# Adaptive max-pooling over rows in a ring: one VectorE instruction per three-row load instead of one per row

## Chip, cores and metric

The kernel runs on one core of one Trainium2 chip. The metric is device time in microseconds (us) of that core. A run over 1.5% above the fastest of its kernel is called slow, the others fast.

## Reference

The input has 32 x 256 rows of 4096 fp32 numbers. Every row is cut into 256 windows of 16, and the maximum of each window is the output: 134.2 MB are read and 8.4 MB written.

```python
def reference(x, output_size):          # x: (32, 256, 4096), output_size = 256
    result = np.zeros((batch, channels, output_size), dtype=np.float32)
    for i in range(output_size):
        start = int(i * length / output_size)
        end = int((i + 1) * length / output_size)
        result[:, :, i] = np.max(x[:, :, start:end], axis=-1)
    return result
```

## The kernel before

Each of the 128 partitions handles 64 rows. 63 of them come in 21 loads of three rows (6 MB over all partitions); the last comes alone in a 2 MB load. The rows go round a ring with nine slots, so three loads fit: one being pooled, two in flight or queued. The results stay on the chip in three `outs` tiles and are stored at the end. Everything except the last small store is issued by one queue (SP), in program order. A load that reuses slots waits, before it is issued, for the pooling that read those slots.

```python
    RING = 9
    G = 21
    N_GROUPS = 3
    LOAD = 3
    CUT = 15
    # ... (tiles ring [P, RING, O, W] and outs[0..2] [P, G * O]; views xg, og, xl, ol)

    def pooled(dst, src):
        nc.vector.reduce_max(out=dst, in_=src, axis=mybir.AxisListType.X)

    n_read = 0
    for g in range(N_GROUPS):
        for r in range(0, G, LOAD):
            at = n_read % RING
            nc.sync.dma_start(
                out=ring[:, at : at + LOAD], in_=xg[g][:, r : r + LOAD]
            )
            for i in range(LOAD):
                pooled(outs[g][:, (r + i) * O : (r + i + 1) * O], ring[:, at + i])
            n_read += LOAD

    at = n_read % RING                    # 63 % 9 = 0: first slot of a trio
    spare = ring[:, (at + LOAD) % RING].rearrange("p o w -> p (o w)")[:, 0:O]
    nc.sync.dma_start(out=ring[:, at], in_=xl)
    pooled(spare, ring[:, at])

    for g in range(N_GROUPS - 1):
        nc.sync.dma_start(out=og[g], in_=outs[g])
    for a, b in ((0, CUT), (CUT, G)):
        nc.sync.dma_start(
            out=og[N_GROUPS - 1][:, a * O : b * O],
            in_=outs[N_GROUPS - 1][:, a * O : b * O],
        )
    nc.scalar.dma_start(out=ol, in_=spare)
```

## Time and profile before

| What | Before |
|---|---|
| time, median of the first 3 runs | 335.93 us |
| VectorE busy | 278.8 us, 83% of the span |
| one load to the next | 14.53 us |
| pooling of one load, three instructions | 13.07 us |
| VectorE idle before each load's pooling | 1.46 us |
| DMA in the steady stretch | share 1.00, 433 GB/s |

First the page of the kernel before: busy time by engine (DVE is VectorE), the DMA engines' busy share in 40 equal slices in tenths (9 is 90% or more), the DMA queue of the loads and stores with its share of 16 engines' span, the chain of waits that ended last, and from the list of DMA issues the median time from issue to landing in the last column.

```profile
DVE 278.8 (83%) x64; POOL 0.2 (0%) x4
...
DMA  9899999999999999999999999999999999999997
...
q1 hardware_dynamic: 3744, 142.48, 98.9%
...
DMA 68%; DVE 26%; DVEq 2%; SPq 0%; issue 0%
...
ring<-in_x_dram SPq DMA_DIRECT2D x21, 6144.0 KB, 30.5
out_dram<-out SPq DMA_DIRECT2D x2, 2688.0 KB, 38.4
ring<-in_x_dram SPq DMA_DIRECT2D x1, 2048.0 KB, 29.5
out_dram<-out SPq DMA_DIRECT2D x1, 1920.0 KB, 38.2
out_dram<-out SPq DMA_DIRECT2D x1, 768.0 KB, 11.2
```

The table by windows, one stretch (length, VectorE busy and GpSimd busy with the number of instructions, TensorE clock, DMA share, GB/s):

```profile
18.44:279.99 261.55, 235.28 (x54) 0.00 (x0) 1.00 1.00 433
```

The timeline (start, duration, engine, line, operation, result and source, number of instructions merged into the line; in brackets the idle time before it and what ended that; SPq is the queue of SP, which issues the DMAs):

```profile
47.48 13.07 DVE L53 TENSOR_REDUCE out<-ring 128x256 f32<-128x4096 f32 x3 [1.47 <-DMA ring<-in_x_dram]
62.01 13.07 DVE L53 TENSOR_REDUCE out<-ring 128x256 f32<-128x4096 f32 x3 [1.45 <-DMA ring<-in_x_dram]
...
284.44 0.33 SPq L68 DMA_DIRECT2D ring<-in_x_dram  x1
284.82 0.90 SPq L72 DMA_DIRECT2D out_dram<-out  x2
293.09 29.40 SPq L74 DMA_DIRECT2D out_dram<-out  x2
...
309.06 13.07 DVE L53 TENSOR_REDUCE out<-ring 128x256 f32<-128x4096 f32 x3 [1.46 <-DMA ring<-in_x_dram]
322.05 4.41 DVE L53 TENSOR_REDUCE ring<-ring 128x256 f32<-128x4096 f32 x1
```

How to read them together: VectorE is busy most of the time, but before every load's pooling it waits for data. The DMA engines, on the other hand, never stop, and 433 GB/s is their pace: the Trainium skill, "DMA: Bandwidth & Descriptors", section "Where 436 GB/s comes from", puts the ceiling of the 16 ports at 435 GB/s. The same section holds a limit of about 358 GB/s per core at HBM for the binding one on such transfers; this trace, with one core at work, does not show it.

The 26% of VectorE in the chain needs care. The chain goes back from each load's landing to the pooling that allowed its issue. But a load lands 30.5 us after its issue, and its own transfer takes only 14.53 us. The rest it spends behind other loads.

### The profile page before, as it was taken

How to read it: one execution, taken by the hardware profiler on the slowest of the kernel's cores; microseconds unless marked ns; L12 is line 12 of the kernel's file. 1: busy time of each engine (PE TensorE's matmuls, PEld its weight loads, DVE VectorE, ACT ScalarE, POOL GpSimd, SP SyncE). 2: the span in 40 equal slices, each digit the busy share in tenths (PEclk: the TensorE clock that was granted, in tenths of full speed). 3: DMA queues.
4: the chain of work that ended last, by engine and by line, in shares of the span. 5: the costliest groups of instructions: out<-in, count | busy, mean ns of one | idle time of the engine just before them, and what ended most of it. 6: DMA issues, size and time to landing. Idle time of an engine off the chain costs nothing.

```text
span 334.3 us, 157 instructions
## 1 busy us (share of the span) xinstructions
DVE 278.8 (83%) x64; POOL 0.2 (0%) x4
## 2 busy tenths in 40 slices
DVE  0078989898898989889898898989889898988990
POOL 0000000000000000000000000000000000000000
DMA  9899999999999999999999999999999999999997
GB/s 371 382 465 453 400 465 394 453 459 394 465 394 453 459 394 465 394 453 459 394 465 394 453 459 394 465 394 448 459 400 459 400 447 459 400 459 388 437 426 297
DMA packets 3889, 142.62 MB, mean 427 GB/s; under 512 B 432, under 2 KB 560, under 8 KB 688
## 3 DMA queue, kind: packets, MB, share of 16 engines
q1 hardware_dynamic: 3744, 142.48, 98.9%
q10 hardware_dynamic: 144, 0.13, 0.1%
q14 instruction: 1, 0.01, 0.0%
HBM read 134.22 MB, written 8.39 MB: 427 GB/s over the span
## 4 chain that ended last, share of the span: by engine, by line
DMA 68%; DVE 26%; DVEq 2%; SPq 0%; issue 0%
DMA ring<-in_x_dram 68%; DVE out L53 25%; DVEq L109 2%; DVE ring L53 1%; SPq L59 0%
## 5 line engine op out<-in xcount | busy, mean ns | idle before, releaser
L53 DVE TENSOR_REDUCE out<-ring 128x256 f32<-128x4096 f32 x63 | 274.5, 4412 | 47.6 <-DMA ring<-in_x_dram 47.6
L53 DVE TENSOR_REDUCE ring<-ring 128x256 f32<-128x4096 f32 x1 | 4.4, 4410 | 0.0
L95 POOL MEMSET const-bfloat16-1.0<- 128x1 bf16 x1 | 0.1, 101 | 0.0
L95 POOL MEMSET const-uint8-127<- 128x1 uint8 x1 | 0.1, 101 | 0.0
L95 POOL MEMSET const-float32-0.0<- 128x1 f32 x1 | 0.1, 98 | 0.2 <-issue 0.2
L95 POOL MEMSET const-float32-1.0<- 128x1 f32 x1 | 0.1, 98 | 0.0
## 6 DMA issues: line engine op xcount, KB each, us to landing
ring<-in_x_dram SPq DMA_DIRECT2D x21, 6144.0 KB, 30.5
out_dram<-out SPq DMA_DIRECT2D x2, 2688.0 KB, 38.4
ring<-in_x_dram SPq DMA_DIRECT2D x1, 2048.0 KB, 29.5
out_dram<-out SPq DMA_DIRECT2D x1, 1920.0 KB, 38.2
out_dram<-out SPq DMA_DIRECT2D x1, 768.0 KB, 11.2
out_dram<-ring ACTq DMA_DIRECT2D x1, 128.0 KB, 6.4
```

Source lines behind the costliest of these rows:

```text
L53: nc.vector.reduce_max(out=dst, in_=src, axis=mybir.AxisListType.X)
L95: nc = _bacc.Bacc("TRN2", target_bir_lowering=False, num_devices=1)
L109: with _tile.TileContext(nc) as tc:
```

## The change

The intent is to save VectorE's fixed cost per instruction: a three-row load lands as a whole and its rows are contiguous in the ring and in `outs`, so one instruction can pool all of it.

```diff
-            for i in range(LOAD):
-                pooled(outs[g][:, (r + i) * O : (r + i + 1) * O], ring[:, at + i])
+            pooled(
+                outs[g][:, r * O : (r + LOAD) * O],
+                ring[:, at : at + LOAD].rearrange("p r o w -> p (r o) w"),
+            )
```

## The prediction

> **What bounds the kernel.** The DMA. The page's DMA row shows nine tenths or more in nearly every slice; q1 holds 98.9% of the 16 engines' span. In the table by windows the steady stretch (18.44 to 279.99 us) has a DMA share of 1.00 at 433 GB/s. VectorE is busy 278.8 us (83%) and idles about 1.46 us before each load's pooling until the load lands (the waits: 47.6 us in 21 times, 18.4 of it the start). The timeline shows one load every 14.53 us, and 13.07 us for its three pooling instructions.
>
> The chain of waits gives VectorE 26%, but that does not make it a limit. A load is issued when the pooling of its slots ends, and lands 30.5 us later, because two loads stand ahead of it: one with 1.46 us left, one of 14.53 us. So it is issued about 16 us before the engines need it.
>
> **What the change does.** 63 pooling instructions of 128x4096 become 21 of 128x12288; the single last row keeps its own. Bytes, loads, stores and buffers stay. The Trainium skill, "VectorE: DVE Perf Modes", section "The TRN2 errata", says that a fixed cost is paid per instruction, so that a large tile pays it once; its Specifications give 0.96 GHz. One short instruction took 4.409 us, against 4096/0.96 = 4.267 us, so 0.142 us is fixed; back to back they start every 4.33 us, so each join costs only 0.063 us. My estimate for the long one is 12288/0.96 + 142 ns = 12.94 us, against 13.07 us for three: 0.13 us per load, 2.7 us of VectorE time in all (278.8 to about 276.1).
>
> **What it moves.** Every steady load waits for the last of its three poolings before and after, so its issue comes 0.13 us earlier. One coarsening: the final one-row load overwrites only the first slot of a trio, and before it waited for that row alone (issued at 284.44 us). Now it waits for the whole trio: issued at about 292.95 us, 8.5 us later, and the two big stores behind it in the queue (284.8 and 285.3) move to about 293.3 and 293.8. The first store of the third group no longer waits of its own.
>
> **How much is on the critical path.** Neither. The load ahead of the final one lands at 309.06 us, so the late issue still has 16 us of queued DMA in front of it. At the end, the last 0.77 MB store is issued at 322.2 us, when pooling allows it, but the 1.92 MB store before it lands at about 331.3; the queue still holds 9 us of work, so 0.13 us from VectorE buys nothing. Bytes set the end.
>
> **Prediction.** 335.9 us, range 335.4 to 336.5; faster by over 2% 0.01, within 2% 0.98, slower by over 2% 0.01.
>
> **What would show it.** Pooling x21 at about 12.94 us; VectorE idle before each rising from 1.46 to about 1.59 us; loads still landing every 14.53 us; DMA share still 1.00 in the steady stretch; the final load's time to landing falling from 29.5 to about 21 us, the big stores' from 38.4 to about 30, with landing times unchanged; the last store still landing about 11 us after its issue.
>
> **What would make it wrong.** A long reduction slower per element than the short one: only above 14.5 us per load would VectorE become the limit. A late issue that leaves some of the 16 engines dry: only if engines ran a load apart, which the even landings speak against. Or a DMA rate that depends on how stores interleave with the last loads; then the tail alone would change, by a microsecond or so.

## The result

| | Before | After |
|---|---|---|
| median (lowest to highest) of 6 runs | 335.94 us (335.76 to 336.12) | 335.75 us (335.42 to 335.96) |
| pooling of one load | 13.07 us | 12.95 us |
| VectorE idle before it | 1.46 us | 1.58 us |
| final load issued, then landed | 284.4, 313.9 us | 292.9, 313.8 us |

The ratio is 0.9995 with a 95% interval of 0.9982 to 1.0007: no difference that these runs could resolve. Ratios here and below are the mean time of one kernel's fast runs over that of the other's fast runs of the same rounds, so they are not quite the ratios of the medians.

The page after:

```profile
DVE 276.3 (83%) x22; POOL 0.2 (0%) x4
...
DMA  9899998999989999899998999989999899998997
...
q1 hardware_dynamic: 3744, 142.48, 98.9%
...
DMA 69%; DVE 25%; DVEq 4%; SPq 0%; issue 0%
...
ring<-in_x_dram SPq DMA_DIRECT2D x21, 6144.0 KB, 30.6
out_dram<-out SPq DMA_DIRECT2D x2, 2688.0 KB, 29.9
ring<-in_x_dram SPq DMA_DIRECT2D x1, 2048.0 KB, 20.9
out_dram<-out SPq DMA_DIRECT2D x1, 1920.0 KB, 37.0
out_dram<-out SPq DMA_DIRECT2D x1, 768.0 KB, 11.3
```

The same stretch of the table by windows after:

```profile
18.44:279.99 261.55, 233.14 (x19) 0.00 (x0) 1.00 1.00 433
```

The timeline after:

```profile
47.41 12.95 DVE L53 TENSOR_REDUCE out<-ring 128x768 f32<-128x12288 f32 x1 [1.58 <-DMA ring<-in_x_dram]
61.95 12.95 DVE L53 TENSOR_REDUCE out<-ring 128x768 f32<-128x12288 f32 x1 [1.58 <-DMA ring<-in_x_dram]
...
292.91 0.33 SPq L70 DMA_DIRECT2D ring<-in_x_dram  x1
293.29 0.90 SPq L74 DMA_DIRECT2D out_dram<-out  x2
294.23 28.07 SPq L76 DMA_DIRECT2D out_dram<-out  x2
...
308.99 12.95 DVE L53 TENSOR_REDUCE out<-ring 128x768 f32<-128x12288 f32 x1 [1.58 <-DMA ring<-in_x_dram]
321.86 4.41 DVE L53 TENSOR_REDUCE ring<-ring 128x256 f32<-128x4096 f32 x1
```

VectorE did become 2.5 us less busy in all. What each load's pooling saved came back as idle time: 12.95 + 1.58 = 14.53 us, and before 13.07 + 1.46 = 14.53 us. The final one-row load is issued 8.5 us later, for a reason the diff does not show: it overwrites only the first slot of a trio, and it now has to wait for the instruction that reads all three. Its time to landing shrinks by the same amount (29.5 to 20.9 us), because it had only been standing in the queue.

### The profile page after: what moved, and what is told of

It reads as the page before. It is cut to its first block, busy times and chain, and to the rows that moved or that the text cites. A ratio compares the mean times of both kernels' runs of the same rounds, so it can differ in the third digit from the quotient of the medians.

```text
span 334.2 us, 115 instructions
## 1 busy us (share of the span) xinstructions
DVE 276.3 (83%) x22; POOL 0.2 (0%) x4
## 4 chain that ended last, share of the span: by engine, by line
DMA 69%; DVE 25%; DVEq 4%; SPq 0%; issue 0%
DMA ring<-in_x_dram 69%; DVE out L53 25%; DVEq L111 4%; SPq L59 0%
## 5 line engine op out<-in xcount | busy, mean ns | idle before, releaser
L53 DVE TENSOR_REDUCE out<-ring 128x768 f32<-128x12288 f32 x21 | 272.0, 12953 | 49.9 <-DMA ring<-in_x_dram 49.9
## 6 DMA issues: line engine op xcount, KB each, us to landing
out_dram<-out SPq DMA_DIRECT2D x2, 2688.0 KB, 29.9
ring<-in_x_dram SPq DMA_DIRECT2D x1, 2048.0 KB, 20.9
out_dram<-out SPq DMA_DIRECT2D x1, 768.0 KB, 11.3
```

## The experiments

Two theories were set against each other.

- **Theory A**: the bytes set the time. About 16 us of queued transfers stand in front of every newly issued load, so neither the saved 0.12 us nor the 8.5 us of lateness reaches the end.
- **Theory B**: both effects count and cancel. VectorE's saving is worth its 2.5 us, as its quarter of the chain suggests, and the later final load and stores give it back. The total alone cannot tell B from A.

### coarse_only: only the later final load

The kernel before, with the final load put into the third slot of its trio, so that it waits for all three row instructions.

```diff
-    nc.sync.dma_start(out=ring[:, at], in_=xl)
-    pooled(spare, ring[:, at])
+    nc.sync.dma_start(out=ring[:, at + 2], in_=xl)
+    pooled(spare, ring[:, at + 2])
```

> The kernel before with one edit: the final one-row load goes into the third slot of its trio, so that it must wait for all three poolings, as it does after the change; pooling stays row by row. Theory A (the DMA queue is the limit, with about 16 us of queued work ahead of every load): final load issued at about 293 us instead of 284.4, its time to landing about 21 us instead of 29.5, total within 0.3 us of the kernel before (335.9). Theory B (VectorE's saving of 2.7 us counts, as its quarter of the chain suggests, and the later final load and stores give it back): 2 to 3 us slower than before, about 338.5.

Measured: 335.97 us against 335.95, ratio 1.0001 (0.9988 to 1.0015). The page shows that the issue did move: the final load (second line) and the big stores (first line) landed about 8.7 us sooner after their issue, as in the changed kernel.

```profile
out_dram<-out SPq DMA_DIRECT2D x2, 2688.0 KB, 29.8
ring<-in_x_dram SPq DMA_DIRECT2D x1, 2048.0 KB, 20.8
```

The lateness alone costs nothing that these runs could resolve. Theory B expected 2 to 3 us. (One load of the profiled run, the longest of the five, came 0.39 us late long before the final load; the section on pieces12_half returns to it.)

### fine_last: only the long instructions, the final load early again

The changed kernel, with the one trio that the final load overwrites pooled by rows.

```diff
-            pooled(
-                outs[g][:, r * O : (r + LOAD) * O],
-                ring[:, at : at + LOAD].rearrange("p r o w -> p (r o) w"),
-            )
+            if n_read == 54:
+                for i in range(LOAD):
+                    pooled(outs[g][:, (r + i) * O : (r + i + 1) * O], ring[:, at + i])
+            else:
+                pooled(
+                    outs[g][:, r * O : (r + LOAD) * O],
+                    ring[:, at : at + LOAD].rearrange("p r o w -> p (r o) w"),
+                )
```

> The changed kernel with one edit: the trio that the final load overwrites is pooled row by row, so that the final load is issued at about 284.4 us again; the other twenty trios keep one instruction. Theory A: 335.8 us, within 0.3 us of both kernels. Theory B: the saving shows without its price, 2 to 2.5 us faster than before, about 333.4.

Measured: 335.91 us, ratio to before 0.9998 (0.9985 to 1.0010). From its timeline:

```profile
265.21 12.95 DVE L53 TENSOR_REDUCE out<-ring 128x768 f32<-128x12288 f32 x1 [1.59 <-DMA ring<-in_x_dram]
...
284.18 0.33 SPq L74 DMA_DIRECT2D ring<-in_x_dram  x1
```

The long instructions are there, the final load was issued at 284.18 us again, and still nothing was gained. Both halves of the change are worth nothing on their own, so theory B falls: there is nothing to cancel.

### half_pool: fifty times the saving

The changed kernel with VectorE's work cut to half; the results are wrong, the transfers are the same.

```diff
-                ring[:, at : at + LOAD].rearrange("p r o w -> p (r o) w"),
+                ring[:, at : at + LOAD, :, 0 : W // 2].rearrange("p r o w -> p (r o) w"),
```

> The changed kernel, but each long instruction reads only the first 8 of every 16 elements (results wrong on purpose; same loads and stores): VectorE falls from 12.95 to about 6.54 us per load (6144/0.96 + 142 ns), 134 us less in all, fifty times what the change saved. Theory A (bytes set the time): the period stays 14.53 us, VectorE's idle before each load grows to about 8 us; total 335.5 to 336 (the last pooling ends earlier, but the stores still queue behind the DMA). Theory B (a quarter of the chain is VectorE's): clearly faster, under 320.

Measured: 336.04 us, ratio to before 1.0000 (0.9985 to 1.0015). From its timeline:

```profile
280.01 6.55 DVE L53 TENSOR_REDUCE out<-ring 128x768 f32<-128x6144 f32 x1 [7.98 <-DMA ring<-in_x_dram]
...
315.53 4.41 DVE L53 TENSOR_REDUCE ring<-ring 128x256 f32<-128x4096 f32 x1
```

The loads still come every 14.53 us (6.55 + 7.98). At the end VectorE is done 6.3 us earlier than in the changed kernel (319.9 instead of 326.3 us) and the span is the same to 0.1 us, so the tail is set by queued bytes too. This is the plainest evidence for theory A: taking away half of VectorE's time changes nothing.

### pieces12 and pieces48: where the joins begin to count

The other direction: each row is pooled in 4 pieces (12 instructions per load) or in 16 (48 per load).

```diff
             for i in range(LOAD):
-                pooled(outs[g][:, (r + i) * O : (r + i + 1) * O], ring[:, at + i])
+                for c in range(0, O, O // 4):          # pieces48: O // 16 throughout
+                    pooled(
+                        outs[g][:, (r + i) * O + c : (r + i) * O + c + O // 4],
+                        ring[:, at + i, c : c + O // 4],
+                    )
```

> The other direction: twelve instructions of 1024 elements per load instead of three or one. With 0.063 us per join and 12.95 us for one, VectorE needs 12.95 + 11 x 0.063 = 13.64 us per load, still under the 14.53 us of a load. Theory A: idle before each load about 0.9 us, total 336. Theory B: 21 x 0.57 = 12 us slower than before, in proportion to the joins.

> Forty-eight instructions of 256 elements per load: 12.95 + 47 x 0.063 = 15.9 us by the same sum, more than the 14.53 us of a load, so that VectorE becomes the limit: theory A expects the period to rise to 15.9 us, VectorE's idle between loads to vanish, and 18.4 + 21 x 15.9 + 4.4 + 3 us of last stores + 1.7 us of launch = about 361 us (357 to 366). If the join costs more than 0.063 us for such short instructions, more. It shows at what VectorE time the joins begin to count.

Measured: pieces12 336.98 us, ratio 1.0026 (1.0009 to 1.0043); pieces48 356.41 us, ratio 1.0607 (1.0591 to 1.0623). The timeline of pieces48 runs 1008 instructions without a gap:

```profile
18.29 329.37 DVE L53 TENSOR_REDUCE out<-ring 128x16 f32<-128x256 f32 x1008 [18.29 <-DMA ring<-in_x_dram]
```

That is 329.37 / 1008 = 0.327 us per instruction or 15.68 us per load, above 14.53, and now the kernel is as slow as its VectorE. In pieces12 the twelve take 13.61 us; eleven joins more than one long instruction add 0.66 us, so a join costs 0.060 us. pieces48 came out under the 357 us at the low end of my range for two reasons. My 0.063 us per join was 5% too much. And I started from the 12.95 us that one long instruction takes alone; in a run without gaps the end of each overlaps the start of the next (in light_whole, below, they start every (244.43 - 12.95) / 18 = 12.86 us). Together that is 0.23 us per load, or 4.8 us over 21 loads.

pieces12 brought a surprise: 1.0 us slower, where theory A said nothing and theory B 12 us. Its timeline shows a single late load; all others before it came every 14.5 us.

```profile
207.38 13.61 DVE L53 TENSOR_REDUCE out<-ring 128x64 f32<-128x1024 f32 x12 [0.92 <-DMA ring<-in_x_dram]
221.91 13.61 DVE L53 TENSOR_REDUCE out<-ring 128x64 f32<-128x1024 f32 x12 [0.92 <-DMA ring<-in_x_dram]
237.41 13.61 DVE L53 TENSOR_REDUCE out<-ring 128x64 f32<-128x1024 f32 x12 [1.88 <-DMA ring<-in_x_dram]
```

### pieces12_half: thin slack, or instruction fetches?

The DMA records of pieces12 hold two instruction fetches of 8 KB in mid-run, at 66 and 227 us. The kernel before has one, the changed kernel none. The lists of queues of pieces12 and of the kernel before (number of packets, MB, share):

```profile
q14 instruction: 2, 0.02, 0.0%
...
q14 instruction: 1, 0.01, 0.0%
```

Next to each, one 48 KB data packet took about 2.47 us instead of 1.82. The experiment keeps the instruction count and halves the data (results wrong).

```diff
-                        ring[:, at + i, c : c + O // 4],
+                        ring[:, at + i, c : c + O // 4, 0 : W // 2],
```

> Why was pieces12 1.0 us slower, although VectorE still waited for every load? Its trace shows one load 1 us late, and two 8 KB instruction fetches on the DMA engines in mid-run (the kernel before has one, the changed one none), each with one data packet of 2.47 us in place of 1.82 beside it. Here the same number of instructions runs on half the data (results wrong on purpose), so that VectorE has some 7 us to spare per load. If the fetches cost the microsecond: again about 337.0, with one late landing. If VectorE's thin slack (0.9 us) did: 336.0, as half_pool.

Measured: 336.98 us, ratio 1.0029 (1.0016 to 1.0043), with over 7 us of VectorE slack:

```profile
221.81 7.21 DVE L53 TENSOR_REDUCE out<-ring 128x64 f32<-128x512 f32 x12 [7.32 <-DMA ring<-in_x_dram]
237.18 7.21 DVE L53 TENSOR_REDUCE out<-ring 128x64 f32<-128x512 f32 x12 [8.16 <-DMA ring<-in_x_dram]
```

So slack is not the cause. The late load follows the second fetch (at 226.6 us) here too: the fetches share the DMA engines with the data, and the microsecond goes with them.

Why the first fetch costs next to nothing and the second one does was not tested by an experiment of its own, but the traces show it. The records do not name the engine of a packet, yet every load has 16 records of 4 bytes, read here as the ends of the 16 engines' shares: VectorE starts 0.4 to 0.5 us after the last of them. A fetch sets one engine back by about 0.97 us (its own 0.32 us and 0.65 us on the packet beside it). Up to the first fetch, the last engine ends 0.76 us (pieces12) or 0.68 us (pieces12_half) after the next. The first fetch sets back one of the others: it then ends 0.06 us after the former last one in pieces12 and 0.15 us before it in pieces12_half, so that the delay is almost hidden. By these ends, the second fetch hits that same engine, and the load is late: VectorE's wait grows by 0.96 us (0.92 to 1.88) and by 0.84 us (7.32 to 8.16). A single fetch can cost time too, where the engine that it hits is not far enough ahead. In the kernel before, that engine still ends 0.05 us before the last; in coarse_only it had only 0.59 us in hand, and the load after the fetch (at 226.1 us) made VectorE wait 1.85 us instead of 1.46:

```profile
236.63 13.07 DVE L53 TENSOR_REDUCE out<-ring 128x256 f32<-128x4096 f32 x3 [1.85 <-DMA ring<-in_x_dram]
```

### ring6_rows and ring6_whole: the queue made thin

If 16 us of queued work are what hides the change, taking them away should uncover it. The two kernels with a ring of six slots have only one load ahead of a newly issued one.

```diff
-    RING = 9
+    RING = 6
```

> The kernel before with a ring of 6 rows instead of 9: one load instead of two stands ahead of a newly issued one, so a load is issued only 1.46 us before the load ahead of it lands. In the trace of before the first DMA packet starts about 1.2 us after the issue began, so the slack is nearly gone: theory A expects from 0 to 0.5 us lost per load in the worst of the 16 engines, 336 to 346 us in all, and a period of 14.5 to 15.0 us between loads. Under theory B, in which the depth of the queue plays no part, 336.

> The changed kernel with a ring of 6. Theory A: if ring6_rows lost time between loads, each issue here comes 0.13 us earlier and up to 0.13 us per load, 2.5 us in all, is now gained over ring6_rows; if ring6_rows lost nothing (slack still enough), both are 335.8 to 336.0. The final load is issued at about 307.5 us, 1.5 us before the load ahead lands, so the tail may lose up to 1 us. Theory B: the same as ring6_rows.

Measured: ring6_rows 363.16 us, ratio to before 1.0802 (1.0779 to 1.0825); ring6_whole 363.96 us, ratio 1.0834 (1.0816 to 1.0851). The cost was 27 us, far more than the at most 10 us I had expected, and the saving in pooling did not show: ring6_whole is not faster than ring6_rows, it is if anything 0.3% slower. Those two intervals overlap, so that difference is not resolved.

The profile of ring6_rows fell on a slow run (367.65 us, 1.7% above that kernel's fastest; the ratio leaves it out), so ring6_whole's is shown, from a fast run. Its page and its timeline:

```profile
DVE 276.4 (76%) x22; POOL 0.2 (0%) x4
...
q1 hardware_dynamic: 3744, 142.48, 95.3%
...
DMA 56%; DVE 40%; issue 0%
```

```profile
205.30 12.95 DVE L53 TENSOR_REDUCE out<-ring 128x768 f32<-128x12288 f32 x1 [2.22 <-DMA ring<-in_x_dram]
222.56 12.95 DVE L53 TENSOR_REDUCE out<-ring 128x768 f32<-128x12288 f32 x1 [4.31 <-DMA ring<-in_x_dram]
237.93 12.95 DVE L53 TENSOR_REDUCE out<-ring 128x768 f32<-128x12288 f32 x1 [2.42 <-DMA ring<-in_x_dram]
```

The loads come unevenly, 15.4 to 17.3 us apart in these lines. The span grew from the changed kernel's 334.2 to 363.0 us. From the queue's shares, the engines idled 4.7% of 363.0 = 17.1 us instead of 1.1% of 334.2 = 3.7 us, and were busy 345.9 us instead of 330.5 us for the same bytes. So about half of the loss is engines with nothing to do, and half is slower packets. In the records 24% of the 48 KB packets took over 1.83 us here (one in a hundred over 2.9 us, the longest 3.7 us), against 0.6% in the changed kernel, all of them at its start. Why a packet takes longer here is not shown. My estimate had counted only the first half. With the loads jumping by up to two microseconds from one to the next, 0.12 us could not show.

### ring6_half: is it the thin queue or the small ring?

ring6_whole with half the pooling (the edit of half_pool; results wrong), so that the same six slots leave about 8 us between a load's issue and its turn.

> The ring of 6 that cost 27 us, with pooling cut to half (results wrong on purpose), so that a load is issued about 8 us before the load ahead lands, in place of 1.5 us. If the loss was for want of queued work in front of the 16 engines (theory A), the period returns to 14.5 us and the time to 336 to 338. If the smaller ring itself costs (fewer buffers, other addresses), it stays near 363.

Measured: 335.88 us, ratio to before 0.9996 (0.9981 to 1.0011). Its table by windows:

```profile
200.00:280.00 80.00, 33.16 (x6) 0.00 (x0) 1.00 1.00 433
```

Share and rate are back at 1.00 and 433 GB/s. The small ring costs nothing by itself; being issued too short a time ahead does. By design the lead was 1.5 us. As the loads came late it grew: it is VectorE's wait before the load ahead, 1.6 to 4.3 us in ring6_whole. Even the load issued 4.31 us ahead landed 15.4 us after the one before it. So the lead that suffices here is at most 8 us, and its lower end is not known; the kernels before and after have 16.

### light_rows and light_whole: the saving where VectorE is the limit

Both kernels with loads cut to 160 of the 256 windows after the ring has been filled once (results wrong; the pooling runs over the whole rows, partly over old data).

```diff
+            n_o = O if n_read < RING else 160
             nc.sync.dma_start(
-                out=ring[:, at : at + LOAD], in_=xg[g][:, r : r + LOAD]
+                out=ring[:, at : at + LOAD, 0:n_o],
+                in_=xg[g][:, r : r + LOAD, 0:n_o],
             )
```

> The kernel before with lighter loads: from the fourth load on, only 160 of the 256 windows of a row are fetched, while the pooling still runs over the whole row in the ring (results wrong on purpose). A load then needs about 9.1 us of DMA and VectorE 13 us, so VectorE is the limit. From the trace (4.33 us start to start, pooling from 18.4 us on without gaps): 18.4 + 63 x 4.33 + 4.4 + 2.3 of last store + 1.7 of launch = 299.6 us (298 to 301).

> The changed kernel with the same lighter loads (results wrong on purpose). If the saving was real and only lay in idle time (theory A), it must now come out in full: 42 joins x 0.063 us = 2.6 us less than light_rows, about 297 us, ratio 0.991. If it comes out as nothing here too, the one long instruction saves nothing that VectorE could use, and the busy time of the profile is misleading.

Measured: light_rows 302.92 us (302.78 to 303.11), light_whole 300.57 us (300.53 to 300.70); from their ratios to before, 0.8946 / 0.9015 = 0.992. Both times are above my sums, by 3.3 and 3.6 us. About 3 us of that are VectorE's two waits before the second and third load, which are still full ones (1.44 + 1.48 us in light_rows); I had forgotten them. The difference is what counts. From the timelines of light_rows and of light_whole:

```profile
47.40 246.71 DVE L53 TENSOR_REDUCE out<-ring 128x256 f32<-128x4096 f32 x57 [1.48 <-DMA ring<-in_x_dram]
```

```profile
47.48 244.43 DVE L53 TENSOR_REDUCE out<-ring 128x768 f32<-128x12288 f32 x19 [1.60 <-DMA ring<-in_x_dram]
```

Nineteen loads without a gap take 2.28 us less, 0.12 us per load, and the kernel is 2.35 us faster. The saving is real and comes out in full once VectorE is the limit. These runs also show the other half of theory A: with fewer bytes, the kernel before falls from 336.01 to 302.92 us although VectorE pools as much. At 0.8% it would still be a small one.

## Why the prediction was right

- **The total.** Predicted 335.9 us, 335.4 to 336.5; measured 335.75 us.
- **What bounds the kernel.** The DMA, with VectorE in waiting: half_pool took half of VectorE's time away and changed nothing.
- **The size of the saving.** 12.94 us was predicted for the long instruction and 12.95 measured; idle 1.59 predicted and 1.58 measured. The sum rested on what the Trainium skill's errata section says, that a large tile pays the fixed cost once. The trace agrees: 12.953 us are 147 cycles over 12288 at 0.96 GHz, and 4.409 us are 137 over 4096.
- **The coarser wait.** Final load issued at 292.91 us (292.95 predicted), time to landing 20.9 us (about 21), big stores 29.9 us (about 30), landing unchanged; coarse_only shows that it costs nothing by itself.
- **The end.** The last store still took 11.3 us from issue to landing. half_pool issued it about 6 us earlier and the span stayed the same.
- **What was off** lies in the experiments' expectations, not in the prediction: the loss with a thin queue was nearly three times the most I allowed, and two instruction fetches could cost a microsecond.

One thing is unresolved: the changed kernel's median is 0.19 us lower, and it has no mid-run instruction fetch while the kernel before has one. The interval includes no change, and the medians of fine_last (no fetch) and coarse_only (one fetch) differ by only 0.06 us, though one fetch did delay a load by 0.39 us in coarse_only's profiled run.

No experiment was made to beat both kernels: at 433 GB/s the 142.6 MB alone take 329 us of the 334 us span, so less than 2% is left to any arrangement that moves the same bytes.

## What to carry to other kernels

Ask first how much work stands queued between the place where you save and the end. Here a load waited 16 us for its turn, so neither 0.12 us less pooling nor 8.5 us more waiting could be seen, although a quarter of the chain ran through VectorE. Check also what else a merge does: it coarsens what later instructions wait for, which is free while the queue is deep; and that depth is worth guarding, as cutting the lead from 16 us to 1.5 us by design cost 27 us.

## What the Trainium skill lacked or had wrong

- "Trainium Kernel Development and Optimization", section "Best Practices", says to double-buffer, and "DMA: Bandwidth & Descriptors", section "Rules for kernel authors", says to issue a DMA early; neither says how early. Here two load buffers with 1.5 us of lead by design (1.6 to 4.3 us measured) ran at 363 and 364 us and three at 336; two with 8 us of lead ran at 336. Beside the idle time, the packets themselves grew slower when the queue ran thin (24% of the 48 KB ones over 1.83 us, against 0.6%). No page has it.
- "VectorE: DVE Perf Modes", section "The TRN2 errata", gives 58 cycles plus one per element and says that it under-predicts a single instruction, for which about 150 cycles were measured. Both figures hold here, for different things: 137 to 147 cycles are the recorded duration's excess, and 58 (0.060 us per join) is what back-to-back `tensor_reduce` instructions add, since each starts about 0.08 us before the recorded end of the one before. That page does not say which to use for a run of instructions; it is the 58: the 57 of light_rows start every (246.71 - 4.41) / 56 = 4.327 us, 58 cycles over 4096. The skill as a whole does not lack this: its page "Perfetto Trace Analysis", section "Optimizing Scalar/DVE Operations", draws the same line between the time on the engine and the longer profiled duration.
- "Runtime: NRT & Kernel Launch", section "Instruction fetch mechanics", calls the cost of crossing a block of instructions mostly hidden. With all DMA engines busy, a kernel with two 8 KB fetches lost 1.0 us, whether VectorE waited 7 us for each load or 0.9 us; by the records, each fetch set one DMA engine back by about 0.97 us. The page gives blocks of 16 KB; the fetches in these traces are of 8 KB.
- "DMA: Bandwidth & Descriptors", section "Where 436 GB/s comes from", says without a condition that HBM, at about 358 GB/s, binds transfers between HBM and the chip's memory. One core alone ran at 433 GB/s here for 260 us. Only that sentence misleads: the same passage has 425 GB/s measured, and the table that this comes from is marked as taken with the pair's other core idle.
